# Hybrid attention, mLSTM and Hyena backbone: zero products at the start, the context's rows loaded behind the modulation's weights, the second layer's Hyena filters made first

## The chip, the cores and the metric

The kernel runs on one core of a Trainium2 chip. A core has five engines with an instruction queue each, worked off in order: TensorE (PE, matrix products into PSUM), VectorE (DVE), ScalarE (ACT), GpSimd (POOL) and SyncE (SP, which here only issues DMAs). The metric is the device time of one execution in microseconds (us), lower is better.

## The reference

Two layers over 1024 latent tokens and 256 context tokens of width 1024. Each layer normalises and modulates the tokens (adaLN), projects them once, runs three groups of mixers side by side, projects back, and ends in a convolutional feed-forward network. The parts that the change touches are the modulation (a product of `silu(c)` with `ada_w`), the first norm, the Hyena filters (a small network with sines over a fixed embedding of time, which does not depend on the tokens), and by its place in the queue the gates of the mLSTM.

```
def rmsnorm(x, g):
    y = x * rsqrt(mean(x * x) + EPS) * g
mods = silu(c) @ ada_w + ada_b                  # shift, scale, gate of each norm
h = rmsnorm(x, g) * (1 + scale) + shift         # input of the shared projection
p = h @ w_in                                    # attention | mLSTM | Hyena
filt = sin(freq * (sin(freq * (emb @ w1 + b1)) @ w2 + b2)) @ w3 * window
filt = filt / sum(|filt|)                       # layer L, class of times
x = x + gate * (concat(mla(p), mlstm(p), hyena(p, filt)) @ w_out)
x = x + gate * conv_ffn(norm(x))
```

## The kernel before

Features lie on partitions, tokens on columns, in three blocks: 0 and 1 of 512 latent tokens, 2 of 256 context tokens. A float32 product is carried by three passes on TensorE (`mm3`): values and weights are split into a high and a low part (`wh` and its low half; the pair `B` for tokens), so a tile of 128 features over 8 tiles of the width is 24 products.

The program is written as one sequence, and a scheduler that simulates the engines' times puts every instruction in its place on its engine's queue. What it writes there is fixed: each engine works its queue in order, and an instruction that waits holds up all behind it. `later(by)` gives the filters a priority of some instructions behind their place, so that they fill gaps.

The run begins with `xT` (8 tiles of 128 x 1280, latent and context columns, in tiles `S`) and the constants. Then the modulation of the first norm: 8 groups (4 `nb`, 2 `half`) of four weight tiles of 256 KB in tiles `B` (`ada`, DMA at line 360): 16 products `a<-B,c_cs` (line 365), a copy by ScalarE (`adarow`, 368), small transpositions `a<-c_sel,adarow`, and the sum with the bias by VectorE (`mods`, 373). The last group also gives the scale `A` (376). Beside this, sums of squares (`nacc`, `nsq`) are collected and turned into 1/rms (`rs_v`, `rs_s`, `rs_r`), which `rs_d` and a product `pj<-rs_d,c_ones` spread over the partitions (`nrb`).

`norm` then makes the tiles `B` of each block: two VectorE operations (453, 456) and one of ScalarE (455) for each of 8 tiles. `mixers_in(L)` runs the filters (`filters`, 477; six or four sines of seven steps, 459), the low-rank projection of the queries (tiles Q0 to Q2; products `pk<-B,wh` and `pj<-B,wh`), then the projection MISC, the gates of the mLSTM (`ml_gates`: `mlLI`, `mlLF`, `mlRR`, `mlast`, `mlmrow`, `mldg`, `mlE`, tiles of a pool `rg`), and by heads V and O (`by_token`, products `pk<-wh,B`). The products of the filters are `f<-zemb,hw`, `f<-sn_h,hw` and `f<-hw,sn_h`, their taps `ft` go to DRAM. The pools of the phases follow one another round the same memory.

Of the kernel before, what the change touches and what calls it, by code (L numbers as in the profile page):

```python
# [9 lines left out]
F32 = mybir.dt.float32  # L10
F32R = mybir.dt.float32r
AF = mybir.ActivationFunctionType
ALU = mybir.AluOpType
AX = mybir.AxisListType
PSUM = bass.MemoryType.PSUM
# [7 lines left out]
TP = 1282                     # token axis with a zero after each stream: x 0:1024, 0, ctx 1025:1281, 0  # L23
# [4 lines left out]
# mLSTM heads are kept in the order 0, 2, 1, 3: head i = 2 * half + pair  # L28
HP = [0, 2, 1, 3]
LATER_F = 100                 # priority of the filters, in instructions behind their place  # L30
SBUF_BYTES = 212832            # a partition of SBUF, as far as it is free
# [3 lines left out]
# (first token, columns, stream: 0 latent / 1 context)  # L35
# [3 lines left out]
# --------------------------------------------------------------------------  # L39
# constants that depend on shapes alone  # L40
# --------------------------------------------------------------------------
def _dft(n, step):
    """Cosines and sines of the classes of n times, step apart, at the first n / step frequencies
    k + 1/2 of 2 n: a list of [time, frequency] each."""
# [7 lines left out]
def _consts():  # L52
# [35 lines left out]
    c["dftc"] = np.stack([ec, oc, es, os_, ec.T, oc.T, es.T, os_.T], 1)      # [n][m][k]  # L88
    cs, sn = _dft(NX, 4)
    cl = [0, 2, 1, 3]  # L90
    f = np.stack([np.stack([cs[i], -sn[i] if i == 3 else sn[i]]) for i in cl])      # [class, cs, time, k]
    f = f.reshape(2, 2, 2, 2, 128, 2, 128)                # [pair, class, cs, half, time, kt, k]
    c["dftf"] = f.transpose(5, 0, 4, 1, 2, 3, 6).reshape(2, 2, 128, 1024)
    v = np.stack([np.stack([cs[i].T, sn[i].T]) for i in cl])      # [class, cs, k, time]
    v = v.reshape(2, 2, 2, 2, 128, 256)                   # [pair, class, cs, kt, k, time]
# [4 lines left out]
def _host(inp):  # L100
    """Lay the inputs out for the chip: slices, transposes, replication."""
# [4 lines left out]
    def colmaj(a):                       # [L, n*128] -> [L, 128, n]  # L106
        return a.reshape(a.shape[0], -1, 128).transpose(0, 2, 1)
# [22 lines left out]
    st = np.stack([cols[n] for n in T_TILES], 1)             # [L, tile, D, 128]  # L130
    o["win"] = st.reshape(L, 14, 8, 128, 128).transpose(0, 1, 3, 2, 4).reshape(L, 14, 128, 1024)
    vo = np.stack([w[:, :, 928:1184], w[:, :, 1184:1440]], 1)  # [L, 2, D, 256]
# [20 lines left out]
    def conv(cw, cb):                    # [L,3,C],[L,C] -> [L,128,C/128,4]  # L153
        a = np.concatenate([cw, cb[:, None]], 1)
        return a.reshape(L, 4, -1, 128).transpose(0, 3, 2, 1)
# [4 lines left out]
    qk = np.zeros((L, 2, 2, 128, 128), np.float32)           # [L, pair, q/k, in, out]  # L160
# [9 lines left out]
    o["hyv"] = np.stack([g["hy_b1"], g["hy_b2"], g["hy_sin_freq"]], -1)   # [L,64,3]  # L170
# [3 lines left out]
    wo = wo.reshape(L, 8, 128, 8, 128)               # [L, k, p, m, c]  # L174
    o["wout"] = wo.transpose(0, 3, 2, 1, 4).reshape(L, 8, 128, 1024)
    up = g["ffn_w_up"].reshape(L, 8, 128, 2, N_FF, 128)      # [L, k, p, ab, j, c]
# [13 lines left out]
class Kern:  # L190
# [30 lines left out]
    def rewind(self):  # L221
        """The next pool at the start of the memory that the phases share: the pools follow one
        another round it, so an unused one takes up what is left. No other pool is open there."""
# [19 lines left out]
    def later(self, by):  # L243
        """Scheduled as if traced `by` instructions later: work that fills gaps."""
# [9 lines left out]
    def mm3(self, out, lh, ll, rh, rl, start, stop):  # L254
        """One K tile of a float32 product carried by three float32r passes."""
# [4 lines left out]
    def ps(self, shape=(128, 512)):  # L260
        """The next of the two banks that all phases share."""
# [9 lines left out]
    def bpair(self, b):  # L271
        """hi and lo of one block of tokens; the context block carries a zero at each end."""
# [1416 lines left out]
```

## Time and profile before

| | |
|---|---|
| three runs | 3817.67 us median (3814.6 to 3827.63) |
| the profiled execution | span 3828.4 us, from first to last instruction; the runs beside it took 3814.6 to 3827.63 |
| TensorE | 3547.6 us busy, 93% of the span; mean granted clock 0.961 |
| VectorE, ScalarE, GpSimd | 2001.4, 1294.6 and 923.9 us busy (52%, 34%, 24%) |
| DMA | 319.46 MB, mean 83 GB/s |

Times in the rows below are those of this one execution, from the span's start. Busy shares are means over stages with different bounds; what a stage costs is read in its own windows. In a timeline, the bracket is the engine's idle time just before the instruction, and what ended it. In the names of the order below, the last number tells tiles of one name apart.

### The profile page before, as it was taken

The numbers are of one execution on the slowest core, as the hardware profiler recorded it, in microseconds if no ns is written. First come the engines' busy times: TensorE is split into PE (matmuls) and PEld (weight loads), VectorE is DVE, ScalarE is ACT, GpSimd is POOL, SyncE is SP. The second block draws the span as 40 slices with busy tenths as digits, with TensorE's granted clock in tenths as the row PEclk, the third lists the DMA queues.
The fourth block names the chain that finished last, engine by engine and source line by source line (L and its number), as shares of the span: only waits on it lengthen the run. The fifth ranks groups of instructions, "written<-read, shape, count | busy, mean of one in ns | idle before, by whom it ended". The sixth has DMA issues, their size and how long they took to land.

```text
span 3828.4 us, 45926 instructions
## 1 busy us (share of the span) xinstructions
PE 3547.6 (93%) x17696; PEld 2809.5 (73%) x17696; DVE 2001.4 (52%) x3037; ACT 1294.6 (34%) x2108; POOL 923.9 (24%) x782
## 2 busy tenths in 40 slices
PE   5999869989899999999999799978999999999997
PEld 3798755556677888888888678856666778888885
DVE  5646675445565433434334765566666543444345
ACT  4433314445543221212112443324566432222222
POOL 1402442222311111111112141143334122222221
PEclk8999989989999999999999899889999999999998
DMA  5322544466242111111111222343232311111111
GB/s 176 115 69 90 198 130 141 126 168 170 71 138 66 39 34 39 39 33 34 39 39 39 94 95 88 108 141 105 54 84 80 102 44 44 45 55 45 44 50 66
DMA packets 195007, 319.46 MB, mean 83 GB/s; under 512 B 32207, under 2 KB 112160, under 8 KB 194788
## 3 DMA queue, kind: packets, MB, share of 16 engines
q1 hardware_dynamic: 194244, 316.23, 26.6%
q8 instruction: 139, 2.28, 0.3%
q14 instruction: 80, 0.66, 0.1%
q0 software_dynamic: 544, 0.31, 0.0%
HBM read 263.50 MB, written 52.81 MB: 83 GB/s over the span
## 4 chain that ended last, share of the span: by engine, by line
PE 59%; DVE 6%; DMA 3%; ACT 2%; issue 2%; POOL 1%; SPq 0%; DVEq 0%; ACTq 0%; POOLq 0%
PE u L252 29%; PE pk L252 12%; PE pj L252 12%; PE st L252 2%; PE pv L252 2%; PE hf L252 1%; ACT wh L300 1%; PE mi L252 0%; DVE B L456 0%; DMA vst<-Ph 0%; PE sm L252 0%; DVE sa L453 0%; PE mo L252 0%; DMA B<-mix 0%; DVE S L1515 0%
## 5 line engine op out<-in xcount | busy, mean ns | idle before, releaser
L252 PE MATMUL u<-B,wh 128*128 128x512 f32 (+1 forms) x3240 | 727.0, 376 | 17.6 <-ACT wh L300 10.6
L252 PEld LDWEIGHTS u<-B,wh 128*128 128x128 f32 x3240 | 573.9, 189 | 141.3 <-ACT wh L300 12.7
L301 POOL TENSOR_TENSOR wh<-wr,wh 128x1024 fp32r<-128x1024 f32 x92 | 222.3, 2416 | 1116.1 <-ACT wh L300 1116.1
L300 ACT CAST wh<-wr 128x1024 fp32r<-128x1024 f32 (+2 forms) x188 | 188.8, 1005 | 775.9 <-PE u L252 425.8
L252 PE MATMUL u<-B,wx 128*128 128x512 f32 (+1 forms) x2040 | 435.1, 367 | 2.3 <-DVE sa L1469 2.3
L252 PEld LDWEIGHTS u<-B,wx 128*128 128x128 f32 x2040 | 352.6, 189 | 70.9 <-issue 2.5
L252 PE MATMUL pj<-B,wh 128*128 128x512 f32 (+1 forms) x1644 | 381.8, 378 | 16.2 <-DVE wh L301 7.0
L252 PE MATMUL pk<-B,wh 128*128 128x512 f32 (+1 forms) x1485 | 355.9, 386 | 31.9 <-ACT S L588 7.8
L252 PEld LDWEIGHTS pj<-B,wh 128*128 128x128 f32 x1644 | 288.5, 193 | 83.6 <-issue 11.9
L252 PEld LDWEIGHTS pk<-B,wh 128*128 128x128 f32 x1485 | 265.7, 197 | 102.2 <-issue 15.3
L1515 DVE SCALAR_TENSOR_TENSOR S<-pk,mods,S 128x512 f32<-128x512 f32 (+1 forms) x220 | 152.7, 694 | 322.5 <-PE pk L252 322.3
L1344 POOL TENSOR_TENSOR Pl<-P,Ph 128x512 fp32r<-128x512 f32 (+1 forms) x168 | 219.4, 1306 | 405.9 <-ACT Ph L1343 349.1
L1515 DVE SCALAR_TENSOR_TENSOR S<-pj,mods,S 128x512 f32<-128x512 f32 (+1 forms) x220 | 152.7, 694 | 307.9 <-PE pj L252 307.8
L252 PE MATMUL st<-qh,S 96*128 96x512 f32 (+1 forms) x960 | 292.7, 411 | 15.1 <-DMA qh<-mr 7.9
L1308 DVE TENSOR_REDUCE mx<-sm 128x1 f32<-128x512 f32 (+1 forms) x400 | 227.6, 588 | 116.4 <-PE sm L252 114.1
L1468 DVE SCALAR_TENSOR_TENSOR sa<-u,ffc,sa 128x1281 f32<-128x1281 f32 (+1 forms) x88 | 124.3, 1413 | 276.3 <-ACT sa L1467 275.0
L1342 ACT ACTIVATE P<-st 128x512 f32<-128x512 f32 (+1 forms) x336 | 197.9, 590 | 162.0 <-PE st L252 82.4
L252 PE MATMUL pk<-g,wh 128*128 128x512 f32 (+1 forms) x1032 | 242.2, 370 | 7.7 <-ACT g L283 3.6
L252 PE MATMUL pj<-g,wh 128*128 128x512 f32 (+1 forms) x1032 | 245.1, 370 | 2.7 <-POOL wh L301 1.6
L252 PEld LDWEIGHTS st<-qh,S 96*128 96x128 f32 (+1 forms) x960 | 183.0, 196 | 75.0 <-DMA qh<-mr 12.2
L252 PE MATMUL pv<-Ph,B 128*64 128x512 f32 (+2 forms) x672 | 213.1, 398 | 12.7 <-ACT Ph L1343 8.4
L252 PEld LDWEIGHTS pk<-g,wh 128*128 128x128 f32 x1032 | 179.6, 189 | 43.8 <-DVE S L1515 4.2
(391 smaller groups left out, 5048.5 us busy)
## 6 DMA issues: line engine op xcount, KB each, us to landing
B<-in_adaw_dram SPq DMA_DIRECT2D x192, 256.0 KB
wr<-in_wup_dram SPq DMA_DIRECT2D x88, 512.0 KB
wr<-in_wdn_dram SPq DMA_DIRECT2D x50, 512.0 KB
wr<-in_wout_dram SPq DMA_DIRECT2D x40, 512.0 KB
wr<-in_win_dram SPq DMA_DIRECT2D x28, 512.0 KB
S<-in_xT_dram SPq DMA_DIRECT2D x16, 640.0 KB
mlrb<-rrows SPq DMA_DIRECT2D x36, 256.0 KB
B<-mix SPq DMA_DIRECT2D x32, 256.0 KB
```

Of the source, the lines that this page charges most:

```text
L252: self.nc.tensor.matmul(out, lhsT, rhs, start=start, stop=stop)
L300: self.nc.scalar.copy(hi, wr)
L301: (self.nc.gpsimd if self.wpool else self.nc.vector).tensor_tensor(lo, wr, hi, op=ALU.subtract)
L1308: nc.vector.reduce_max(st["mx"][:, qt, bi:bi + 1], ps[:, :kn], axis=AX.X)
L1342: nc.scalar.activation(P[:, :n], ps[:, :n], AF.Exp, scale=SCALE)
L1344: (nc.gpsimd if j % 2 else nc.vector).tensor_tensor(Pl[:, :n], P[:, :n], Ph[:, :n], op=ALU.subtract)
L1468: nc.vector.scalar_tensor_tensor(y[:, 1:W], pu[:, 0:W - 1], cw[:, 0:1], y[:, 1:W], op0=ALU.mult, op1=ALU.add)
L1515: nc.vector.scalar_tensor_tensor(x, ps, self.mods[L][:, 40 + m, s:s + 1], x, op0=ALU.mult, op1=ALU.add)
```

## The change

- `xT` is loaded in two parts: the latent columns first, the context's columns behind all 32 weight tiles of the modulation, on the same queue.
- `filters(1)` is made at the beginning, ahead of the modulation in the program, with its DMAs on GpSimd's queue and three of each sine's seven steps on GpSimd. `filters(0)` stays in `mixers_in(0)`, but uses the same tiles (pool `rf`), so it comes after `filters(1)`. `mixers_in(1)` has no filters.
- 70 products of a tile of zeros (`wu<-ntmp`) stand ahead of the modulation, and for 7 of the 8 groups two products of ones with the last two of the group's four weight tiles (`wu<-B,c_ones`, 128x256). Nothing reads `wu`.
- In PSUM the modulation has three banks instead of six, the filters two, `wu` one.

```diff
+WARM = 70
...
-    def sine(self, ps, n, freq, b, sp):
+    def sine(self, ps, n, freq, b, sp, eng):
...
-        nc.vector.tensor_scalar(k[:, :n], a[:, :n], 1.0 / (2.0 * math.pi), magic, op0=ALU.mult, op1=ALU.add)
-        nc.vector.tensor_scalar(k[:, :n], k[:, :n], -magic, None, op0=ALU.add)
+        eng.tensor_scalar(k[:, :n], a[:, :n], 1.0 / (2.0 * math.pi), magic, op0=ALU.mult, op1=ALU.add)
+        eng.tensor_scalar(k[:, :n], k[:, :n], -magic, None, op0=ALU.add)
...
-        nc.vector.tensor_scalar(a[:, :n], a[:, :n], 3.1415925, -3.1415925, op0=ALU.min, op1=ALU.max)
+        eng.tensor_scalar(a[:, :n], a[:, :n], 3.1415925, -3.1415925, op0=ALU.min, op1=ALU.max)
...
-    def filters(self, L, sp, pp, tag):
+    def filters(self, L, sp, pp, tag, eng, dma):
...
     def mixers_in(self, L):
-            fp = self.pool(e, f"pf{L}", PSUM, f0=2, ap=1)
-            with ExitStack() as e1, self.later(LATER_F):
-                rp = self.pool(e1, f"rf{L}", sn_a=1, sn_k=1, sn_h=1, hw1=1, hw2=1, hw3=1, hv=1, fb=2, fab=1, ft=1,
-                               fl1=1, fls=1, win=2, zemb=1)
-                self.filters(L, rp, fp, "f0")
+            fp = self.pool(e, f"pf{L}", PSUM, f0=2 if L == 0 else 1, ap=1)
+            if L == 0:
+                with self.erf, self.later(LATER_F):
+                    self.filters(L, self.rf, fp, "f0", nc.vector, nc.sync)
...
     def run(self):
-                nc.sync.dma_start(x[:, :T], a["xT"][k])
+                nc.sync.dma_start(x[:, :NX], a["xT"][k][:, :NX])
...
-                pp = self.pool(e0, "p0", PSUM, a0=6)
+                self.rf = self.pool(e0, "rf", sn_a=1, sn_k=1, sn_h=1, hw1=1, hw2=1, hw3=1, hv=1, fb=2, fab=1,
+                                    ft=1, fl1=1, fls=1, win=2, zemb=1)
+                pp = self.pool(e1, "p0", PSUM, a0=3, f0=2, wu=1)
+                self.hsc = [self.t(self.cp, [128, 2, 2], f"c_hsc{L}") for L in range(DEPTH)]
+                self.filters(1, self.rf, pp, "f0", nc.gpsimd, nc.gpsimd)
+                z = self.t(rp, [128, 512], "ntmp", F32R)
+                nc.gpsimd.memset(z.bitcast(F32), 0.0)
+                wu = self.t(pp, [128, 512], "wu")
+                for i in range(WARM):
+                    self.mm(wu, z[:, 0:128], z)
                 for nb in range(4):
                     for half in range(2):
-                        self.ada(0, nb, half, lambda: self.blk(dt=F32), pp, "a0")
+                        ws = self.ada(0, nb, half, lambda: self.blk(dt=F32), pp, "a0")
+                        for w in ws[2:] if (nb, half) != (3, 1) else ():
+                            self.mm(wu[:, 0:256], self.ones, w[:, 1])
+                for k in range(8):
+                    nc.sync.dma_start(xs[k][:, NX:T], a["xT"][k][:, NX:T])
```

Three places of TensorE's queue. The first is in the modulation, around the products of group 2 (the third of eight). Before, the transposition of a group (`a<-c_sel,adarow`) stands between its products and the next group's:

```order
L252 MATMUL a_38_259<-c_sel_187,adarow_257 128x2 x2
L365 MATMUL a_39_263<-B_270,c_cs_184 32x256 x2
L365 MATMUL a_39_263<-B_268,c_cs_184 32x256 x2
L365 MATMUL a_39_263<-B_266,c_cs_184 32x256 x2
L365 MATMUL a_39_263<-B_264,c_cs_184 32x256 x2
L252 MATMUL pk_516<-c_ones_191,nacc_493 128x2 x4
L252 MATMUL a_45_282<-c_sel_187,adarow_280 128x2 x2
L365 MATMUL a_46_286<-B_293,c_cs_184 32x256 x2
```

Now the products of ones on the weights of groups 5 and 6 (`wu<-B_611`, then `wu<-B_634` and `wu<-B_636`; group 6 has the tiles `B_630` to `B_636`) stand behind group 2's products:

```order
L366 MATMUL a_108_529<-B_536,c_cs_184 32x256 x2
L366 MATMUL a_108_529<-B_534,c_cs_184 32x256 x2
L366 MATMUL a_108_529<-B_532,c_cs_184 32x256 x2
L366 MATMUL a_108_529<-B_530,c_cs_184 32x256 x2
L253 MATMUL wu_408<-B_611,c_ones_191 128x256
L253 MATMUL wu_408<-B_634,c_ones_191 128x256
L253 MATMUL wu_408<-B_636,c_ones_191 128x256
L253 MATMUL a_114_548<-c_sel_187,adarow_546 128x2 x2
L366 MATMUL a_115_554<-B_561,c_cs_184 32x256 x2
L366 MATMUL a_115_554<-B_559,c_cs_184 32x256 x2
L366 MATMUL a_115_554<-B_557,c_cs_184 32x256 x2
L366 MATMUL a_115_554<-B_555,c_cs_184 32x256 x2
```

What moved: behind group 2's products TensorE now takes up weights of group 6, before group 2's transposition and before the products of group 3 (`B_555` to `B_561`) and of all later groups.

The second place is the first projection of layer 0, at the end of the 24 products of tile Q0 on block 0. Before, the products of Q0 and Q1 (there `pk_990` and `pj_1017`) alternate as the tiles `B` come, both to their end:

```order
L252 MATMUL pj_1017<-B_482,wh_986 128x512
L252 MATMUL pj_1017<-B_481,wh_987 128x512
L252 MATMUL pj_1017<-B_487,wh_986 128x512
L252 MATMUL pk_990<-B_488,wh_980 128x512
L252 MATMUL pk_990<-B_487,wh_981 128x512
L252 MATMUL pj_1017<-B_488,wh_986 128x512
L252 MATMUL pj_1017<-B_487,wh_987 128x512
L252 MATMUL f_217_746<-sn_h_744,hw_209_724 64x512
```

Now:

```order
L253 MATMUL pk_1269<-B_765,wh_1260 128x512
L253 MATMUL pk_1269<-B_771,wh_1259 128x512
L253 MATMUL f_66_330<-sn_h_328,hw_28_223 64x512
L253 MATMUL pk_1269<-B_772,wh_1259 128x512
L253 MATMUL pk_1269<-B_771,wh_1260 128x512
L253 MATMUL pj_905<-rs_d_903,c_ones_191 128x256
L253 MATMUL pj_1296<-B_729,wh_1265 128x512
L253 MATMUL pj_1296<-B_730,wh_1265 128x512
```

What moved: the product that spreads the context's 1/rms (`pj_905<-rs_d_903`) stands between Q0 (`pk_1269`) and Q1 (`pj_1296`) of block 0.

The third place is in the gates of layer 0, from the last maxima to the first product of the states. Before, rows of V and O stand between the steps, as here behind the second small product on `mldg`; the first product on `wqk` comes 31 rows later:

```order
L252 MATMUL pk_2280<-wh_2270,B_463 128x256
L252 MATMUL pk_2280<-wh_2271,B_463 128x256
L252 MATMUL pk_2280<-wh_2270,B_464 128x256
L252 MATMUL pk_2280<-wh_2276,B_469 128x256
L252 MATMUL mm_1562<-mldg_1566,c_ones_191 128x128
L252 MATMUL pj_2308<-wh_2270,B_445 128x256
L252 MATMUL pj_2308<-wh_2271,B_445 128x256
L252 MATMUL pj_2308<-wh_2270,B_446 128x256
L252 MATMUL pj_2308<-wh_2270,B_451 128x256
```

Now:

```order
L253 MATMUL mm_1767<-c_ident_189,mlLI_1762 64x128
L253 MATMUL mm_1767<-c_ntri_966,mlLF_1761 64x128 x2
L253 MATMUL mm_1767<-c_ident_189,mlLI_1762 64x128
L253 MATMUL mm_1767<-c_ntri_966,mlLF_1761 64x128
L253 MATMUL mm_1802<-c_ident_189,mlast_1797 1x128 x2
L253 MATMUL mm_1828<-c_ones_191,mlmrow_1807 128x2
L779 MATMUL mm_1836<-c_ident_189,mlRR_1774 128x128 x3
L253 MATMUL mm_1841<-mldg_1842,c_ones_191 128x128
L253 MATMUL mm_1841<-mldg_1845,c_ones_191 128x128
L253 MATMUL mm_2346<-wqk_1872,S_1962 128x128
L253 MATMUL mm_2346<-wqk_1872,S_2057 128x128
L253 MATMUL pk_2615<-wh_2549,B_729 128x256
```

What moved: the products of V and O that stood between the steps are now ahead of them, and from `mm_1767` to `mm_2346` the gates' own products follow one another directly.

## Rows read from the trace of the kernel before

**Rows 1.** Windows: busy us by engine, granted clock, DMA share, GB/s.
```profile
40.00:45.00 5.00, 5.00 (x25) 2.65 (x25) 3.25 (x11) 2.70 (x8) 0.00 (x0) 1.00 1.09 361
```

**Rows 2.** Timeline of PE: start, us, instructions, idle before.
```profile
28.13 1.94 PE L365 MATMUL a<-B,c_cs 128*32 128x256 f32 x16 [5.74 <-DMA B<-in_adaw_dram]
...
47.95 1.07 PE L365 MATMUL a<-B,c_cs 128*32 128x256 f32 x16
...
55.33 0.61 PE L252 MATMUL a<-c_sel,adarow 128*128 128x2 f32 x4 [0.57 <-ACT adarow L368]
```

**Rows 3.** Timeline of DVE around the scale A.
```profile
56.17 0.17 DVE L376 SCALAR_TENSOR_TENSOR A<-mods,ng 128x16 f32<-128x16 f32 x1
...
57.40 2.73 DVE L453 SCALAR_TENSOR_TENSOR ntmp<-S,A,nrb 128x512 f32<-128x512 f32 x4
```

**Rows 4.** Groups of DVE, 58 to 92 us: busy, mean ns.
```profile
L456 DVE SCALAR_TENSOR_TENSOR B<-ntmp,mods,B 128x512 fp32r<-128x512 f32 x16 | 11.3, 738 | 0.0
L453 DVE SCALAR_TENSOR_TENSOR ntmp<-S,A,nrb 128x512 f32<-128x512 f32 x16 | 11.2, 740 | 0.0
...
L469 DVE SCALAR_TENSOR_TENSOR sn_a<-sn_k,sn_a 64x512 f32<-64x512 f32 x5 | 3.4, 677 | 0.0
```

**Rows 5.** Windows of the norm.
```profile
76.00:80.00 4.00, 0.68 (x2) 0.19 (x2) 4.00 (x7) 3.37 (x5) 0.00 (x0) 1.00 0.00 0
```

**Rows 6.** Timeline of PE, layer 0's projections.
```profile
84.84 8.66 PE L252 MATMUL pk<-B,wh 128*128 128x512 f32 x24 [4.45 <-ACT S L588]
...
97.62 1.98 PE L252 MATMUL f<-hw,sn_h 64*128 64x512 f32 x4
...
110.47 5.75 PE L252 MATMUL pk<-B,wh 128*128 128x512 f32 x24
...
169.79 7.21 PE L252 MATMUL pj<-B,wh 128*128 128x512 f32 x24
```

**Rows 7.** Waits of PE, 56 to 300 us: total, times, longest.
```profile
PE f L252 <- ACT sn_h L472: 7.7, 2, 4.0
```

**Rows 8.** Windows, layer 0's gates.
```profile
198.00:228.00 30.00, 29.47 (x246) 28.41 (x245) 14.31 (x57) 7.28 (x13) 1.05 (x2) 1.00 0.16 49
```

**Rows 9.** Timeline of PE, layer 1's gates.
```profile
2278.18 1.40 PE L713 MATMUL mm<-c_ident,S 16*128 16x16 f32 x20
...
2302.08 0.38 PE L252 MATMUL mm<-c_ones,mlmrow 1*128 1x2 f32 x2
...
2306.91 1.22 PE L252 MATMUL mm<-wqk,S 128*128 128x128 f32 x4 [1.10 <-DVE mlE L792]
```

**Rows 10.** Timeline of DVE, layer 1's gates.
```profile
2282.38 0.24 DVE L726 SCALAR_TENSOR_TENSOR mlLF<-mlG,mle 128x80 f32<-128x80 f32 x1 [2.07 <-ACT mle L721]
2285.02 0.42 DVE L738 COPY mlRR<-mm 128x256 f32<-128x256 f32 x1 [2.39 <-PE mm L252]
...
2290.41 0.33 DVE L753 COPY mlast<-mlB 64x1 f32<-64x1 f32 x2
```

**Rows 11.** Timeline of ACT, layer 1's gates.
```profile
2297.23 1.28 ACT L793 ACT_TABLE_LOAD   x1
```

**Rows 12.** Windows 2100 to 2300 us, tile f alone.
```profile
sum 200.00, PE 13.32 PEld 3.79 DVE 8.72; mean PE 4.44 PEld 1.26 DVE 2.91
```

**Rows 13.** Windows of layer 1's beginning, all tiles.
```profile
2100.00:2200.00 100.00, 77.89 (x324) 58.96 (x323) 78.73 (x129) 46.53 (x76) 15.46 (x24) 0.90 0.29 95
2200.00:2250.00 50.00, 47.48 (x206) 33.97 (x206) 38.97 (x46) 21.88 (x31) 26.53 (x24) 0.97 0.40 138
```

**Rows 14.** Waits of PE, 2140 to 2320 us.
```profile
PE f L252 <- ACT sn_h L472: 2.5, 1, 2.5
...
PE mm L252 <- DVE mlE L792: 1.1, 1, 1.1
```

**Rows 15.** Groups of POOL, line 963.
```profile
L963 POOL TENSOR_SCALAR S<-S,c_hyd 128x1280 f32<-128x1280 f32 x2 | 7.3, 3664 | 5.6 <-PE pj L959 5.6
```

**Rows 16.** Groups of DVE, line 600.
```profile
L600 DVE SCALAR_TENSOR_TENSOR S<-S,c_qg,rb 128x512 f32<-128x512 f32 x12 | 12.7, 1101 | 0.0
```

More of the change, by code (lines that the diff above doesn't have):

```diff
@@ L348, in load_consts2 @@
                 nc.gpsimd.dma_start(d[nm], a[nm][L])
-            d["hsc"] = self.t(cp, [128, 2, 2], f"c_hsc{L}")
+            d["hsc"] = self.hsc[L]
             self.lc.append(d)
@@ L377, in ada @@
                                            op0=ALU.add, op1=ALU.mult)
+        return ws
     def inv_rms(self, acc, n, dim, sp, ps):
@@ L484, in filters @@
         hv = self.t(sp, [64, 3], "hv")
-        nc.sync.dma_start(w1, a["hw1"][L])
-        nc.sync.dma_start(w2, a["hw2"][L])
-        nc.sync.dma_start(w3, a["hw3"][L])
-        nc.sync.dma_start(hv, a["hyv"][L])
+        dma.dma_start(w1, a["hw1"][L])
+        dma.dma_start(w2, a["hw2"][L])
+        dma.dma_start(w3, a["hw3"][L])
+        dma.dma_start(hv, a["hyv"][L])
         for blk in (range(3) if L < DEPTH - 1 else range(2)):
@@ L493, in filters @@
             z = self.t(sp, [33, 512], "zemb")
-            nc.sync.dma_start(z[:, :n], a["zemb"][:, c0:c0 + n])
+            dma.dma_start(z[:, :n], a["zemb"][:, c0:c0 + n])
             ps = self.t(pp, [128, 512], tag)
             self.mm(ps[:64, :n], w1, z[:, :n])
-            h = self.sine(ps[:64, :n], n, hv[:, 2:3], hv[:, 0:1], sp)
+            h = self.sine(ps[:64, :n], n, hv[:, 2:3], hv[:, 0:1], sp, eng)
             ps = self.t(pp, [128, 512], tag)
             self.mm(ps[:64, :n], w2, h[:, :n])
-            h = self.sine(ps[:64, :n], n, hv[:, 2:3], hv[:, 1:2], sp)
+            h = self.sine(ps[:64, :n], n, hv[:, 2:3], hv[:, 1:2], sp, eng)
             for i in range(n // 128):
@@ L503, in filters @@
                 win = self.t(sp, [128, 256], "win")
-                nc.sync.dma_start(win, a["hwin"][:, kk])
+                dma.dma_start(win, a["hwin"][:, kk])
                 ps = self.t(pp, [128, 512], tag)
@@ L534, in filters @@
                 nc.vector.reciprocal(v, v)
-                nc.vector.tensor_copy(self.lc[L]["hsc"][:, st], v[:, :, 0])
+                nc.vector.tensor_copy(self.hsc[L][:, st], v[:, :, 0])
     def project(self, L, tiles, blocks):
@@ L1592, in run @@
             self.hs = [{} for _ in range(8)]
-            with ExitStack() as e0:
+            self.erf = e0 = ExitStack()
+            with ExitStack() as e1:
                 rp = self.pool(e0, "r0", nacc=1, nsq=1, ntmp=4, nrb=2, rs_s=2, rs_r=2, rs_v=2, rs_d=1)
-                pp = self.pool(e0, "p0", PSUM, a0=6)
+                self.rf = self.pool(e0, "rf", sn_a=1, sn_k=1, sn_h=1, hw1=1, hw2=1, hw3=1, hv=1, fb=2, fab=1,
[8 more added lines that the diff above has]
+                    self.mm(wu, z[:, 0:128], z)
                 for nb in range(4):
                     for half in range(2):
-                        self.ada(0, nb, half, lambda: self.blk(dt=F32), pp, "a0")
+                        ws = self.ada(0, nb, half, lambda: self.blk(dt=F32), pp, "a0")
[3 more added lines that the diff above has]
+                    nc.sync.dma_start(xs[k][:, NX:T], a["xT"][k][:, NX:T])
                 for b in range(3):
```

## The prediction

> **What bounds the kernel now.** TensorE is busy for nearly the whole span (the table above), so a product that leaves a stretch where TensorE waits for nothing is worth its whole duration, and a product that TensorE does while it would wait anyway costs nothing. The change touches three stretches, and I read them one after the other, first the windows (who is busy), then each engine's timeline (who waits for whom).
>
> The beginning, until 48 us, is bound by the transfer of the first modulation's weights: 361 GB/s with all DMA engines busy [rows 1]. On TensorE the first of eight groups of weight products starts when its weights land, at 28.13 [rows 2]. What the reader is to see there: a group takes 1.94 us at 28.13, but 1.07 at 47.95, the same 16 records. That is the lower of the clock's two levels (1.2 GHz) against the higher (2.4), although the granted clock of this stretch reads 1.00; I go by the durations. TensorE is done with the last transposition at 55.33 + 0.61 = 55.94, and VectorE has the scale `A` at 56.17 [rows 3].
>
> From there to about 92 us VectorE is the bound: it is busy 4.00 of 4.00 us, GpSimd 0.00, TensorE 0.68 [rows 5]; the norm costs it two operations of 0.74 for each 128x512 tile [rows 4]. TensorE works without a break from 84.84 [rows 6].
>
> The gates of layer 0 (198 to 228 us) run through small steps on TensorE, VectorE and ScalarE, and TensorE is busy 29.47 of 30.00 there [rows 8]: V and O products of the heads stand between the steps. The input phase of layer 1 holds its filters, 13.32 us of TensorE [rows 12].
>
> **The change part by part.** *Weights earlier.* The context's 1.05 MB no longer lies ahead of the weights (2.9 us at 361 GB/s [rows 1]), but layer 1's filter data do, some 0.5 MB by its tile sizes (1.5 us). A group of four weights is 1.05 MB, 2.9 us. Before, group 6 of 0 to 7 was in at 28.13 + 6 x 2.9 = 45.5; now, by this, at 44 (43 to 46).
>
> *Zero products and products on weights.* The 70 products on zeros stand ahead of the first weight group, in time that TensorE waits in. They cost nothing unless the first group is delayed; 70 of 128x512 at 0.24 (24 in 5.75 [rows 6]) are 17 us, and the wait for weights is longer. The 14 products on weights are another matter, by the order: two on group 6's weights stand before the transposition of group 2 and before the products of groups 3 to 7. TensorE works in order, so until group 6 has landed it does nothing for those five groups, although their weights are there. From 44 it then owes five groups at 1.07, six transpositions at 0.61, one wait of 0.57 for ScalarE's copy [rows 2], five filter products at 0.99 [rows 6] and about 1.5 for the statistics: 5.4 + 3.7 + 0.6 + 5.0 + 1.5 = 16 us. So the last transposition ends near 60, `A` follows at 61 (before 56.17 [rows 3]): **5 us later** (3 to 8). The warm clock is in this: at the lower level the 16 us would be over 25.
>
> *The context behind the weights.* Its sums of squares and its 1/rms now come after `A`, inside the norm of the latent blocks. In TensorE's order the spreading product `pj_905` of the context stands between Q0 and Q1 of block 0, and waits for VectorE's `rs_d_903`. VectorE has in front of that 29 norm operations at 0.74 [rows 4], three sine steps at 0.68 and some ten small ones: 21.5 + 2.0 + 2.9 = 26.4 us from its first norm operation. That one came 1.2 us after `A` before (57.40 [rows 3]); so 57.4 + 5 + 26.4 = 88.8. Three of seven sine steps go to GpSimd, which idles here [rows 5], and take some 0.4 off VectorE each, but are longer there: 3.66 us for 1280 columns [rows 15], so by estimate 1.5 for 512, thrice in a row per sine. And GpSimd beside VectorE may cost: the same kind of operation as the norm's takes 1.10 instead of 0.74 where other engines work beside it [rows 16]. I take 2 us for this (0 to 8), so Q1 of block 0 starts near 91.3. Before, TensorE ran without a break from 84.84 [rows 6]: 6.5 later, and it still owes Q1 of block 0 (5.75 for 24, in [rows 6]) and six filter products more than before, since layer 0's filters have not begun (5.9): 18.1. Back come the wait for `sn_h` of 4.0 [rows 7] and the cold stretch at 169.79 (7.21 instead of 5.75, [rows 6]): 5.5. **Layer 0's projections lag by 12.5 us** (5 to 22).
>
> The Trainium skill, SBUF — State Buffer, section "Who interferes with whom", says that a VectorE instruction with two inputs in SBUF contends with a GpSimd instruction that reads SBUF, through one shared pair of ports held for the whole instruction. The norm's operations and the sine's subtractions have two such inputs. Rows 16 against rows 4 agree in sign but do not show who worked beside them. By that rule the third rival below would come about.
>
> *Layer 0's gates.* Layer 0's filters now come second in the same buffers and end later, while the V and O products go ahead as before. The gates' tiles lie in the filters' memory and wait for their end. So in the new order most of V and O is done when the gates begin: after the transpositions come 21 V and O rows, and then every step of the gates, one behind another, with nothing between until `wqk`. The chain is to be seen bare in layer 1: 3.0 us from the transpositions' end to `mlLF`, 5.7 from `mlRR` to the last maximum's copy [rows 10], 4.8 from `mlmrow` to the first `wqk` product [rows 9], about 1.3 for the sums between and 5.5 for the row's steps (of 11.3 there, where weight conversions and queued products stood between): 20.3, and 2.3 for the exponential, the output gate and one more table load of 1.28 [rows 11] until the bank is free. Off go 2.5 for the 21 rows (half of 5.75 x 21/24) and 4.5 for the chain's own products: 15.5 us without work. Then the clock is cold: 24 products take 8.66 instead of 5.75 [rows 6], 2.9. **18 us lost** (12 if the first links run ahead, 24 if the whole 27.3 us of layer 1 recur less the 21 rows).
>
> *Layer 1 without filters.* Its products lie where TensorE is busy: 13.3 us off [rows 12], and the wait of 2.5 for `sn_h` [rows 14]. Its gates' four waits, the largest 1.1 [rows 14], 3.2 together, go because V and O now stand around them, and about 1 of the tail: **20 us won** (16 to 25).
>
> Sum: 12.5 + 18 - 20 = +10.5 us. The profiled execution spans 3828.4, 10.7 above the median of the runs, 3817.67; I add the difference to the median: **3828**.
>
> **The rivals.** *Not slower: layer 1 gives more* (faster). In layer 1's beginning TensorE is busy only 77.89 of 100 us and VectorE 78.73 [rows 13]. If VectorE is the bound there, what leaves it (8.7 us that read the filters' products [rows 12], twelve subtractions of 0.68 [rows 4] and smaller steps, about 20) counts too, and layer 1 gives up to 33 instead of 20. With the smaller lag of 5 and a stall of 13 in layer 0's gates that is 5 + 13 - 33 = -15: 3803. It decides where layer 1's gain exceeds the two losses by 11.5: over 29.5 with these, over 42 with the losses as worked out above. Against it: TensorE is busy 47.48 of 50.00 us where most of the filters stand [rows 13], so only the early part can give more.
> *The losses cancel* (same): the lag shrinks to 5 because TensorE's later work had waits to take it up: 5 + 15 - 20 = 0, 3818.
> *GpSimd and VectorE hold each other up* (slower): six to nine GpSimd steps lie within the norm, and each holds it up for its 1.5 us: 9 to 13, of which 2 are in the sum, so about 3837. For it [rows 16], against it that an instruction loses at most the rest of the other's time.
> *The clock falls* while TensorE waits for group 6 (slower): the 16 us become about 26, 3838. The products on weights are there against it; before, the stretch was cold [rows 2].
>
> **How the numbers follow.** What a measurement of this kernel can tell from no change is about 0.3%, 11.5 us, and my sum lies just at that border. I give the forecast 0.52, half on each side of the border; faster 0.21; the losses cancel 0.10; contention 0.09; a cold clock 0.08. So faster 0.21, same 0.36, slower 0.43. The range of 8 in 10 reaches from the faster rival's end to beyond the slower ones: 3801 to 3846; the forecast's own is 3819 to 3838.
>
> **What would show it.** Right: `A` at 60 to 63; TensorE without a break from about 91; one idle stretch of 14 to 20 us in layer 0's gates near 220, with the small products one by one in it; layer 1's beginning 16 to 25 shorter. Wrong, each by itself: `A` before 57 (weights not gating); V and O products between the gates' steps; norm operations over 0.9 (contention); layer 1 shorter by 30.

## The result and the profile after

The changed kernel takes 3855.7 us, median of 4 runs (3840.73 to 3859.08), the kernel before in the 4 runs beside it 3822.61, 33.1 less by these medians. The ratio is 1.0078 (95% interval 1.0061 to 1.0094): **slower by 0.8%**. Its profiled execution, 3838.5 us of span, is the fastest of the four, so one pair of profiles understates the difference. Runs of both kernels unchanged, on other chips (e1, e7, e13, e17, e18 below), give three profiles of the changed kernel and four of before. The times at which TensorE begins certain products divide them into stages:

| stage on TensorE | before, four profiles | changed, three | difference of means |
|---|---|---|---|
| start to first score product (`st`), layer 0 | 534.9, 539.3, 535.3, 535.0 | 577.8, 584.9, 582.3 | +45.6 |
| to first feed-forward product (`u`): attention | 647.6, 639.0, 642.9, 652.6 | 644.1, 656.4, 649.6 | +4.5 |
| to the end of layer 0's last `u` | 988.6, 988.8, 988.7, 989.0 | 990.9, 989.1, 989.1 | +0.9 |
| to first `st` of layer 1 | 414.5, 417.7, 414.5, 412.9 | 384.8, 383.3, 383.3 | -31.1 |
| to TensorE's last product | 1233.5, 1230.2, 1231.7, 1233.7 | 1231.7, 1239.6, 1235.2 | +3.2 |

The sum is +23.1, the difference of the mean spans 22.9; the times by themselves, by the three ratios to before (1.0078, 1.0081, 1.0057), give 22 to 31. Attention differs by more among profiles of one kernel (639 to 653) than between the kernels. So the case is two numbers: 46 lost until layer 0's attention, 31 won at the start of layer 1.

The beginning, TensorE's timeline of the changed kernel's first profile:

```profile
5.83 9.58 PE L253 MATMUL wu<-ntmp 128*128 128x512 f32 x32 [5.83 <-POOL ntmp L1605]
...
25.25 1.07 PE L366 MATMUL a<-B,c_cs 128*32 128x256 f32 x16
...
37.56 1.93 PE L366 MATMUL a<-B,c_cs 128*32 128x256 f32 x16
...
51.20 1.07 PE L366 MATMUL a<-B,c_cs 128*32 128x256 f32 x16
...
62.66 0.61 PE L253 MATMUL a<-c_sel,adarow 128*128 128x2 f32 x4
64.12 1.48 PE L253 MATMUL pj<-rs_d,c_ones 128*128 128x512 f32 x2 [0.85 <-DVE rs_d L399]
78.41 0.98 PE L253 MATMUL pk<-c_ones,nacc 128*128 128x2 f32 x4 [12.81 <-DVE nacc L437]
82.07 6.80 PE L253 MATMUL pk<-B,wh 128*128 128x512 f32 x22 [2.67 <-DVE rs_v L390]
...
95.70 1.22 PE L253 MATMUL pj<-rs_d,c_ones 128*128 128x256 f32 x2 [5.17 <-DVE rs_d L399]
97.38 2.93 PE L253 MATMUL pj<-B,wh 128*128 128x512 f32 x6 [0.46 <-ACT nrb L404]
...
105.32 4.35 PE L253 MATMUL pk<-B,wh 128*128 128x512 f32 x18
```

The zero products run from 5.83 until the first weights are in, and seven of the eight groups take 1.07 (the one at 37.56 takes 1.93; the first in [rows 2] 1.94): in this profile the clock is at its higher level for most of the modulation. Yet the last transposition ends at 63.27 (55.94 in [rows 2]). A product on the context's squares stands ahead of the first projection and waits 12.81 for them. Q0 of block 0 is done at 90.53; then TensorE waits 5.17 for the context's `rs_d`, Q1 of block 0 comes at 97.38, and Q0 of block 1 at 105.32, in [rows 6] at 84.84. VectorE beside it, the scale and the first norm operations:

```profile
67.03 0.15 DVE L377 SCALAR_TENSOR_TENSOR A<-mods,ng 128x16 f32<-128x16 f32 x1
...
67.44 5.30 DVE L455 SCALAR_TENSOR_TENSOR ntmp<-S,A,nrb 128x512 f32<-128x512 f32 x4
```

`A` is 10.9 later than in [rows 3], and the first four norm operations take 5.30, there 2.73. The groups of the norm, with mean ns:

```profile
L455 DVE SCALAR_TENSOR_TENSOR ntmp<-S,A,nrb 128x512 f32<-128x512 f32 x16 | 14.2, 917 | 0.0
L458 DVE SCALAR_TENSOR_TENSOR B<-ntmp,mods,B 128x512 fp32r<-128x512 f32 x16 | 13.4, 868 | 0.0
```

They are 0.92 and 0.87 against 0.74 in [rows 4]: 32 operations, 4.9 us (2.4 in e1 and e17). V and O begin 12.4 later than before, here the first rows of before and of the changed kernel:

```profile
187.38 1.70 PE L252 MATMUL pk<-wh,B 128*128 128x256 f32 x13
```

```profile
199.77 0.99 PE L253 MATMUL pk<-wh,B 128*128 128x256 f32 x7
```

Then the filters of layer 0 that are still owed, and the gates. First the windows from there to the attention, of before and then of the changed kernel: all tiles, then the products of tile `f` alone; behind them the waits of TensorE in the gates:

```profile
187.38:534.90 347.52, 320.84 (x2045) 278.83 (x2044) 220.44 (x392) 109.34 (x221) 103.05 (x110) 0.95 0.35 113
187.38:534.90 347.52, 0.56 (x4) 0.52 (x4) 0.15 (x1) 0.95 0.35 113
```

```profile
199.77:577.79 378.02, 335.07 (x2064) 284.94 (x2063) 237.56 (x421) 118.52 (x233) 118.44 (x125) 0.92 0.33 109
199.77:577.79 378.02, 8.53 (x24) 3.35 (x24) 5.33 (x10) 0.92 0.33 109
```

```profile
PE mm L253 <- DVE mlast L754: 5.9, 1, 5.9
PE mm L253 <- DVE mlmrow L766: 4.0, 1, 4.0
PE f L253 <- POOL fl L521: 2.2, 1, 2.2
PE mm L253 <- DVE mlLF L727: 1.6, 1, 1.6
PE mm L253 <- DVE mlE L793: 1.1, 1, 1.1
PE mm L253 <- DVE mlTT L780: 0.6, 1, 0.6
...
PE mm L253 <- DVE mldg L784: 0.4, 1, 0.4
PE mm L779 <- DVE mlast L769: 0.2, 1, 0.2
```

The gates' waits are 13.9 (5.9 + 4.0 + 1.6 + 1.1 + 0.6 + 0.4 + 0.2, rounded rows), one behind another as the order has them; in [rows 8] TensorE was idle for 0.5 there. Windows of the gates, with the granted clock:

```profile
240.00:290.00 50.00, 36.10 (x303) 32.77 (x304) 23.91 (x81) 12.10 (x25) 5.59 (x13) 0.80 0.24 76
```

So from V and O to the attention, of 30.5 in all: 8.0 of filter products (8.5, before 0.6), 13.9 of waits in the gates, 2.2 of waiting for the filters' sum, and some 6 because the other products run longer (TensorE is busy 14.2 more, of which 8.0 are the filters'), at a granted clock of 0.92 instead of 0.95; in the gates it is 0.80.

In layer 1, from the last products of layer 0's feed-forward to the first score, sums of before and then of the changed kernel:

```profile
sum 436.40, PE 393.42 PEld 323.78 DVE 276.77 ACT 151.04 POOL 121.71; mean PE 131.14 PEld 107.93 DVE 92.26 ACT 50.35 POOL 40.57
```

```profile
sum 406.80, PE 370.24 PEld 313.50 DVE 242.27 ACT 137.75 POOL 95.71; mean PE 123.41 PEld 104.50 DVE 80.76 ACT 45.91 POOL 31.90
```

TensorE is busy 23.2 us less, of which the filters' products are only 13.3 [rows 12]. The other 9.9 are products that run shorter: the windows' granted clock, weighted by their lengths, is 0.93 instead of 0.91. And it is idle 6.4 less (36.6 against 43.0). Both recur: over this stage the granted clock is 0.91 to 0.93 in the four profiles of before, 0.93 to 0.94 in the three of the changed kernel.

### The profile page after: what moved, and what is told of

It is laid out like the page before. It is cut to its first block, busy times and chain, and to the rows that moved or that the text cites. A ratio compares the mean times of both kernels' runs of the same rounds, so it can differ in the third digit from the quotient of the medians.

```text
span 3838.5 us, 46110 instructions
## 1 busy us (share of the span) xinstructions
PE 3566.8 (93%) x17794; PEld 2830.0 (74%) x17794; DVE 2003.0 (52%) x3025; ACT 1297.7 (34%) x2109; POOL 951.5 (25%) x809
## 5 line engine op out<-in xcount | busy, mean ns | idle before, releaser
L253 PEld LDWEIGHTS pk<-B,wh 128*128 128x128 f32 x1485 | 264.7, 197 | 89.7 <-issue 11.1
L253 PE MATMUL pv<-Ph,B 128*64 128x512 f32 (+2 forms) x672 | 214.6, 400 | 12.2 <-ACT Ph L1344 8.2
L253 PEld LDWEIGHTS pj<-g,wh 128*128 128x128 f32 x1032 | 180.6, 189 | 42.2 <-POOL wh L302 5.6
```

What stands on the lines that cost most here:

```text
L253: self.nc.tensor.matmul(out, lhsT, rhs, start=start, stop=stop)
```

## Experiments

Ratios are to the kernel before, run beside them. Edits are to the changed kernel where they say "changed", else to before.

**e1, e17: the changed kernel again; e7, e13, e18: before again.** 

> The changed kernel again, unchanged. Its profiled execution (3840.73 us, clock 0.957) was the fastest of four, the others 3853 to 3859 at 0.954 and 0.955. Theory 'clock': the stalls of the start (about 12 us) and of layer 0's gates (about 16 us) recur within 1 us in every execution, layer 1 gives back 18, and what separates 3841 from 3856 lies in stretches in which TensorE's granted clock falls, attention above all; executions then order by clock. Rival 'start': the slow executions are later already at 300 us, by another 10 to 15 us. Rival 'chance': it comes out at 3825 to 3840 this time and the difference of the medians was chance.

> The changed kernel, unchanged, beside the kernel before on one chip. Sum by stage against the yardstick beside it: first score product +42 to +50, layer 1 from the feed-forward's end to its first score product -28 to -31, so +13 to +20 from these. If the two attentions make up the rest of the 30 us, layer 0's is 6 to 14 us longer than the yardstick's, layer 1's with the feed-forward 3 to 8. If they are equal within 3 us, the rest lies elsewhere or the first difference of medians was too large.

e1: 1.0081 (1.0066 to 1.0096); e17: 1.0057 (1.0037 to 1.0076). Before again gave 0.9993, 0.9988 and 0.9990. The stages are in the table above. On e17's chip, against the yardstick e18 beside it: +47.3 until the scores, -3.0 in attention, -29.6 in layer 1's first part, +1.5 to the end, +16. I had expected an attention 6 to 14 longer; it is not, so a loss in attention is not shown, and by my own condition the rest lies elsewhere or the first difference of medians was too large.

The stretch from V and O to the scores recurs: 378.0, 378.3 and 377.7 us in the three profiles of the changed kernel (347.5 to 352.2 before), with 13.9 to 14.0 of waits in the gates. What varies is the start: V and O begin at 199.8, 206.6 and 204.6 (185.3 to 187.4 before). In e1 the clock falls within the modulation: the last three groups take 1.9 again, and four filter products behind the first of these 3.77 instead of 1.98:

```profile
50.99 1.91 PE L366 MATMUL a<-B,c_cs 128*32 128x256 f32 x16
```

`A` comes at 72.9 there; in e17, where the last two groups take 1.93, at 71.3. Between the first profile and e1 attention differs by 12.3 too, so neither 'clock' nor 'start' alone makes the difference between these two. For before alone I had expected:

> The kernel before, unchanged, for a second profile of it. If the attention of layer 0 (a stretch with many waits and a clock that falls and rises) takes different times in executions of one program, this profile shows it: from the first score product to the first product of the feed-forward 640 to 660 us, where the first profile has 647.5. If it is 647 within 2 us here too, the 656 of the changed kernel's second profile are a consequence of the change. Time 1.000 of before.

Attention spread over 639.0 to 652.6 in one program. A difference of that size between two single profiles says nothing.

**e9: layer 1's filters first, and nothing else but the PSUM banks for them (four for the modulation instead of six).**

```diff
+                self.filters(1, self.rf, pp, "f0", nc.gpsimd, nc.gpsimd)
                 for nb in range(4):
...
+                with self.erf, self.later(LATER_F):
+                    self.filters(L, self.rf, fp, "f0", nc.vector, nc.sync)
```

> The kernel before with layer 1's filters made first (GpSimd steps and DMA queue as in the change), and nothing else: no zero products, no products on weights, the context loaded with the rest. In its order the gates of layer 0 again stand bare behind layer 0's filters. Theory 'filters': this part brings the whole loss in layer 0 (first score product 35 to 43 us later than before) and the whole gain in layer 1 (25 to 30 us); time +10 to +25. Rival 'the rest costs it': without zero products and late context the time is within 5 us of before.

1.0056 (1.0037 to 1.0075), as the whole change. First score at 578.2 (+42 against the mean of before), layer 1's stage 382.9 (-32). Both halves of the result are in this one edit. Its beginning, without zero products, is slower still: `A` at 69.4. GpSimd's sine steps in its timeline:

```profile
22.75 0.61 POOL L468 TENSOR_SCALAR sn_k<-sn_a 64x512 f32<-64x512 f32 x1 [2.94 <-DVE sn_a L465]
23.45 1.51 POOL L469 TENSOR_SCALAR sn_k<-sn_k 64x512 f32<-64x512 f32 x1
...
81.36 5.03 POOL L472 TENSOR_SCALAR sn_a<-sn_a 64x512 f32<-64x512 f32 x1 [8.84 <-DVE sn_a L471]
93.23 4.89 POOL L468 TENSOR_SCALAR sn_k<-sn_a 64x512 f32<-64x512 f32 x1 [6.84 <-DVE sn_a L465]
```

The same step takes 0.61 while VectorE does little (22.75) and 4.89 in the norm (93.23). The Trainium skill, SBUF — State Buffer, section "Who interferes with whom", names the lock that a VectorE instruction with two SBUF inputs and a GpSimd instruction that reads SBUF share; these rows agree, and here it is mostly GpSimd that waits: 5 us in a chain on which layer 0's filters hang. In the changed kernel itself the sine steps take 2.72 at most, and the slowest step of GpSimd is one of the filters' sums, here before the norm and then in it:

```profile
61.72 0.72 POOL L520 TENSOR_TENSOR fl<-fl,fab 128x256 f32<-128x256 f32 x1 [0.46 <-ACT fab L515]
...
74.10 8.42 POOL L520 TENSOR_TENSOR fl<-fl,fab 128x256 f32<-128x256 f32 x1 [3.23 <-ACT fab L515]
```

It recurs with 8.42 in e1 and e17.

**e19: changed, all sine steps on VectorE.**

```diff
-                self.filters(1, self.rf, pp, "f0", nc.gpsimd, nc.gpsimd)
+                self.filters(1, self.rf, pp, "f0", nc.vector, nc.gpsimd)
```

> The changed kernel with all sine steps on VectorE, nothing else changed. In its order layer 0's filters end some 95 rows earlier on TensorE, and 36, 39 and 48 rows stand between the gates' first steps; only the last ones stay bare. If GpSimd's slow steps are what makes the filters late, the idle time in the gates falls from 14 to 4 to 7 us and the first score product comes 8 to 15 us earlier than in the changed kernel: time -8 to -15 against it. If VectorE is the bound of the norm, its added steps (three of 0.4 for each of four sines) delay the norm by as much, and no more than 4 us are won.

1.0029 (1.0017 to 1.0042), 8.9 us below e17's median on the same chip. Waits of TensorE around its gates:

```profile
PE mm L253 <- DVE mlE L793: 1.1, 1, 1.1
PE mm L253 <- DVE mlast L754: 1.1, 1, 1.1
PE mm L253 <- DVE mldg L784: 0.8, 1, 0.8
PE mm L253 <- DVE mlTT L780: 0.7, 1, 0.7
...
PE mm L779 <- DVE mlast L769: 0.3, 1, 0.3
```

4.0 in the gates, not 13.9, and the first score 15.5 earlier than in e17, although `A` comes at 76.5, later than in any other run. V and O begin at 209.2 (204.6 in e17), and from there to the scores it is 357.6 instead of 377.7 (before 349.5 in the mean). So the loss behind V and O goes with the end of layer 0's filters, 28 in e17 and 8 here; the other 23 of this run lie ahead of V and O. Whether the filters end earlier by GpSimd's slow steps or by the other order that the scheduler made of them is not separated.

**e11, e15: layer 0's filters first, layer 1's in their old place, the context's rows ahead of the weights as before; e15 with the zero products and those on weights.** The lines against the changed kernel:

```diff
-                self.filters(1, self.rf, pp, "f0", nc.gpsimd, nc.gpsimd)
+                self.filters(0, self.rf, pp, "f0", nc.vector, nc.gpsimd)
...
             if L == 0:
-                with self.erf, self.later(LATER_F):
-                    self.filters(L, self.rf, fp, "f0", nc.vector, nc.sync)
+                self.erf.close()
+            else:
...
+                    self.filters(L, rp, fp, "f0", nc.vector, nc.sync)
```

> Layer 0's filters made at the beginning (all sine steps on VectorE, DMAs on GpSimd's queue), layer 1's in their old place in layer 1; no zero products, context loaded with the rest. If the late end of layer 0's filters is what bares the gates, V and O products stand between the gates' steps here, the stall of 14 us is gone, and about 9 us of filter products lie in the beginning, where TensorE waits: first score product 5 to 12 us earlier than before, time -4 to -12. Rival: VectorE is the bound of the beginning, the filters' steps delay the norm by their own time, and nothing is gained (0 to +8).

> Layer 0's filters at the beginning and layer 1's in layer 1, as in the run without zero products, now with the 70 products on zeros and the 14 on weights. There the clock was at its lower level from 50 us on, filter products took 1.9 us instead of 1.0, and the scale A came near 73. If the clock is what delays A, A comes at 60 to 66 here and the time falls by 4 to 10 us against that run (which was 5.8 us above before): within 5 us of before. If the filters' chain of waits delays A, it stays over 70 and the time does not fall.

e11: 1.0011 (0.9999 to 1.0023); e15: 0.9993 (0.9981 to 1.0005). In their order V and O stand between the gates' steps again. The waits of TensorE in e11's gates, all that there are:

```profile
PE mm L253 <- DVE mlast L758: 2.1, 1, 2.1
PE pk L253 <- ACT S L680: 0.6, 1, 0.6
PE pk L253 <- DVE wh L302: 0.5, 2, 0.3
PE mm L253 <- DVE mlLF L731: 0.3, 1, 0.3
```

The bared gates are gone, and with them the loss behind V and O: from there to the scores 349.9 and 350.8 (before 349.5). The first score comes at 544.4 and 543.5, 8 and 7 later than before, nearly all of it ahead of V and O. My gain of 5 to 12 at the start did not come: `A` at 73.3, and at 68.3 with zero products, between what the two readings for e15 said. Neither beats before beyond its interval.

**e2: changed, without the products on weights.**

```diff
-                        for w in ws[2:] if (nb, half) != (3, 1) else ():
-                            self.mm(wu[:, 0:256], self.ones, w[:, 1])
```

> The changed kernel without the 14 products on the modulation's weights; the 70 products on zeros stay. If these 14 hold up groups 3 to 7, the scale A comes at 57 to 60 instead of 67 and the time falls by 5 to 9 us against the changed kernel. If they keep the clock up and only that counts, the modulation's groups take 1.9 instead of 1.07 us and A does not come earlier; time unchanged within 4 us. The stall in layer 0's gates (14 us idle) stays in either case.

1.0082 (1.0066 to 1.0098), as e1 beside it. `A` comes at 65.3 instead of 72.9, although from 32.88 on the groups take 1.93: so the products on weights do hold `A` back. Already group 1 starts at 28.99 here, at 37.17 in e1. And nothing is won: TensorE then stands 16.84 at the context's squares, and the first projection starts at 89.4 (88.8 in e1). Rows of TensorE, GpSimd and VectorE:

```profile
85.02 1.01 PE L253 MATMUL pk<-c_ones,nacc 128*128 128x2 f32 x4 [16.84 <-DVE nacc L437]
```

```profile
69.12 7.29 POOL L468 TENSOR_SCALAR sn_k<-sn_a 64x512 f32<-64x512 f32 x1 [4.39 <-DVE sn_a L465]
```

```profile
79.34 1.21 DVE L471 SCALAR_TENSOR_TENSOR sn_a<-sn_k,sn_a 64x512 f32<-64x512 f32 x1 [3.41 <-POOL sn_k L469]
```

A sine step of GpSimd takes 7.29 here, most of it within the norm, and VectorE waits 3.41 for the one behind it. The context's `rs_d` comes only 2.2 earlier than in e1, and Q1 of block 0 with it.

**e6: changed, both filters at their old places. e4: only the context behind the weights.**

> The changed kernel with both layers' filters at their old places (in the input phases, all sine steps on VectorE); zero products, products on weights and the context behind the weights stay. In its order V and O products stand between the gates' steps of layer 0 again. Theory: the gates' stall (16 us) goes, layer 1's gain (about 18 us) goes too, and the start's lag shrinks; so 3825 to 3834 us, 20 us or more below the changed kernel's median. Rival 'start bears it all': the loss stays at 25 us or more.

> The kernel before with nothing but the context's columns loaded behind the modulation's weights. The scale A comes 2 to 4 us earlier (1.05 MB less ahead of the weights), but VectorE collects the context's squares inside the norm of the latent blocks, so the norm ends 2 to 5 us later relative to A. Theory: these cancel, within 5 us of before. Rival: TensorE stands behind the context's statistics, as in the changed kernel (12.8 us of wait there), and layer 0's projections come 6 to 12 us later.

e6: 1.0020 (1.0003 to 1.0036); e4: 1.0017 (1.0002 to 1.0032). Two rows of e6's TensorE timeline:

```profile
49.01 0.61 PE L253 MATMUL a<-c_sel,adarow 128*128 128x2 f32 x4 [0.57 <-ACT adarow L369]
...
70.01 1.01 PE L253 MATMUL pk<-c_ones,nacc 128*128 128x2 f32 x4 [16.32 <-DVE nacc L437]
```

Here zero products, products on weights and late context do what the start of the change seems made for: `A` at 49.9, 6.3 earlier than before. Then TensorE waits 16.32 for the late context, and V and O begin at 187.9 as before. With the filters at their old places both halves of the result are gone: first score at 537.8 (534.9 to 539.3 before), layer 1's stage 414.7. In e4 `A` comes at 61.1, not earlier, and V and O begin 9.6 later than before, as the rival said, but not by its wait: TensorE waits 3.22 and 5.29 for ScalarE's copies in the modulation.

**e5, e14: only the 70 zero products, twice.** 

> The kernel before with nothing but the 70 products on zeros ahead of the modulation (modulation with 5 PSUM banks). If the zero products bring the clock up early, groups of the modulation take 1.07 instead of 1.9 us, but most of that is hidden behind the transfer of the weights: A earlier by 2 to 4 us, time -2 to -4, no change that can be measured. Rival: the clock is down again at the first wait for weights, A at 56 as before, 0 us. Slower by over 5 us would mean that the products stand in the way.

> The kernel before with nothing but the 70 products on zeros, a second time: it was 14 us slower than before the first time, and no stage of its profile up to the attention showed more than 5. If the zeros cost something by what they change in the order of later instructions, the same stages are longer here, against the yardstick beside it: 2 to 6 us in the mLSTM's states, 5 to 12 in layer 0's attention; time +10 to +16. If the first result was chance, within 4 us of before.

1.0038 (1.0024 to 1.0052) and 1.0028 (1.0014 to 1.0043): slower. `A` comes at 59.3 and 56.2, not earlier, as the rival said: the zero products end before the first weights are in, TensorE waits, and the first group is at the clock's lower level again, here in e14:

```profile
26.99 1.93 PE L365 MATMUL a<-B,c_cs 128*32 128x256 f32 x16 [4.96 <-DMA B<-in_adaw_dram]
```

The loss is not where the products are: e14's first score comes 0.8 after its yardstick's, e13. Attention, first score to first `u`, in windows of e13 and then of e14:

```profile
sum 643.00, PE 570.55 PEld 404.62 DVE 350.76 ACT 302.76 POOL 162.70; mean PE 95.09 PEld 67.44 DVE 58.46 ACT 50.46 POOL 27.12
```

```profile
sum 654.00, PE 581.57 PEld 411.69 DVE 348.60 ACT 303.51 POOL 164.53; mean PE 96.93 PEld 68.61 DVE 58.10 ACT 50.59 POOL 27.42
```

11 us more of busy time for the same products, 654 in both runs. But e18, before unchanged, has 652.6 there at the same granted clock, 0.92, so the attention is not shown to be the place. The scheduler has put some later instructions in another order; that this order costs the time was not tried, and e15, with the same zero products, has 639 in attention. Where e5 and e14 lose stays open.

**e12: changed, banks of their own for layer 0's filters.**

```diff
-            fp = self.pool(e, f"pf{L}", PSUM, f0=2 if L == 0 else 1, ap=1)
             if L == 0:
                 with self.erf, self.later(LATER_F):
-                    self.filters(L, self.rf, fp, "f0", nc.vector, nc.sync)
+                    ff = self.pool(self.erf, "pfil", PSUM, f0=2)
+                    self.filters(L, self.rf, ff, "f0", nc.vector, nc.sync)
+            fp = self.pool(e, f"pf{L}", PSUM, f0=1, ap=1)
```

> The changed kernel, with PSUM banks of their own for layer 0's filters, so that the gates' bank is not one that the filters still use. In its order the transpositions stand 28 rows earlier, ahead of the filters' last products, and 31 rows of V and O and the filters stand between them and the next gates' step; from the maxima on the steps stay bare. If the bank alone holds the gates up, the idle time in the gates falls from 14 to 3 us or less; if the filters' memory in SBUF holds them (tiles of the gates lie there), only the first waits go and 8 to 12 us stay. Time against the changed kernel -10, or -2 to -5.

1.0124 (1.0100 to 1.0148), a miss, and worse: now the low-rank queries' products (`ap`) begin at 239.89, directly behind the filters' last at 239.01, so the gates began at 260.8 instead of 243.7 and stayed bare. It says nothing on which of the two memories holds the gates; that stays open.

**e16: before, with layer 1's filters beside layer 0's gates.**

```diff
...
+                if L == 0:
+                    rf = self.pool(e1, "rf1", sn_a=1, sn_k=1, sn_h=1, hw1=1, hw2=1, hw3=1, hv=1, fb=2, fab=1, ft=1,
+                                   fl1=1, fls=1, win=2, zemb=1)
+                    ff = self.pool(e1, "pg1", PSUM, f0=2)
                 self.ml_gates(misc, ra, rg, pp)
+                if L == 0:
+                    with self.later(LATER_F):
+                        self.filters(1, rf, ff, "f0")
```

> The kernel before with layer 1's filters made in layer 0 beside the gates, behind layer 0's own, in memory and banks of their own; beginning as before, no zero products, context with the rest. If the explanation holds (layer 1 gives 28 to 31 us back when its filters are gone, and layer 0 loses because its own filters end late and the gates stand bare), layer 0 loses only the 13 us of products and some 5 to 10 of waits in the filters' chain, and layer 1 gives 28 to 31: time -5 to -15, faster than both kernels. If the gain in layer 1 hung on the other edits, or the gates are bared here too, 0 to +10.

1.0031 (1.0020 to 1.0041), a miss. Layer 1 won its 28 (stage 384.6), but layer 0 lost 33 until the scores: 17 of filter products, not 13, and 14 of waits in the filters' chain, not 5 to 10. The waits:

```profile
PE f L252 <- POOL fl L519: 7.7, 1, 7.7
PE f L252 <- ACT sn_h L472: 6.4, 2, 4.5
```

## Why the prediction was wrong

The direction and the three places were right, the sizes were not: 3828 forecast, 3855.7 measured, outside the range. Of the signs of being wrong that it named, two came: norm operations over 0.9 (0.92, for one of the two kinds) and layer 1 shorter by 30 (31.1).

- *The start.* `A` 5 later: it came 10.9 (first profile) to 16.7 later (e1). The reason given, products on later groups' weights, is real (e2: without them `A` is 7.6 earlier), and TensorE came to group 6's weights at 44.26, as worked out. From there it took 19.0 instead of 16 to the last transposition, and VectorE's steps for the filters and the sums put `A` 3.8 behind that. In e1 and e17 the clock fell on the way, which is the fourth rival in part, though not while TensorE waited for group 6. From VectorE's first norm operation to the end of the context's `rs_d`, 28.2 us, it went as worked out (26.4 and 2 of contention; 57.4, 5 and these make 90.8, and the 0.5 up to the 91.3 of the prediction has no row). The wait for the context's squares ahead of Q0 had no price in the sum; by these rows it costs nothing, since Q1 waits for `rs_d` anyhow.
- *The lag of layer 0's projections*, 12.5: V and O began 12.4 later in the first profile, 17.0 in the mean of three. The 12.4 is luck: Q0 of block 1 was 20.5 late, not 12.2, and 8.1 came back by V and O, where the sum, with 5.9 more owed and 5.5 back, had nothing come back. **This is the step that failed:** I charged six filter products, 5.9, ahead of V and O, and nothing behind, although I had written that layer 0's filters end later. In fact 8.0 us of their products and 2.2 of waiting came behind V and O, on top of the gates, and of the 4.0 us of `sn_h` wait that I gave back, 2.1 stayed.
- *The gates*, 18: 13.9 idle (15.5 forecast) and some 6 by a lower clock (2.9 forecast), about as worked out. e9 alone brings the loss, e6 takes it away, and e11 and e15 show its cause: with layer 0's filters early the long waits are gone, 2.4 us are left in e11 (2.1 + 0.3). That the gates wait for the filters' memory in SBUF, as the prediction has it, is not shown (e12). Until the scores the two terms made +45.6, not 30.5: 17.0 ahead of V and O, 28.5 behind.
- *Layer 1*, 20 won: 31. Products (13.3) and waits (6.4 less idle; 6.7 forecast) were right; 10 us by a higher clock were not in the sum. The first rival's 33 is near in number, but not by its reason, VectorE as the bound: the rows give 23.2 to TensorE's own busy time and 6.4 to its waits.
- *GpSimd against VectorE*, third rival: real, but smaller on VectorE, 4.9 us on the norm's operations in the first profile and 2.4 in e1 and e17, not 9 to 13. GpSimd lost more: its steps of 8.42 beside operations of 0.74 are far over "the rest of the other's time" that the prediction held against this rival.
- The sum of the errors, 15.1 lost and 11.1 won, and 8.6 in stages that vary by as much, is what separates 10.5 from 23, the difference of the mean profiles.

## What to carry to other kernels

Work that is moved into an idle stretch at the front is not free when what follows it uses the same buffers: ask what now ends last there, and which later chain waits for that end. Here the moved filters cost layer 0 more than they gave layer 1, because layer 0's own filters became second, and the gates behind them lost the products that had covered their steps. Where a scheduler sets the order, an edit that should cost nothing in its place can still cost time (e5 and e14), and one pair of profiles does not show where: attention of before alone spreads over 13.6 us. A stage table over several profiles of both kernels is worth more.

## What the runs showed of the hardware

- One GpSimd operation on 64x512 took 0.61 us at 22.75 and 5.03 and 4.89 us in the norm (e9), where the estimate in the prediction was 1.5. One on 128x256 took 0.72 us at 61.72 and 8.42 in the norm (changed kernel, e1, e17).
- The same program's attention took 639.0 to 652.6 us in four profiles of before, at granted clocks from 0.93 (639.0) to 0.92 (652.6).
- Zero products that run until the first weights are in leave the clock at its higher level: the first modulation group took 1.07 us at 25.25 in the changed kernel, 1.94 at 28.13 in [rows 2]. Where 4.96 us of waiting lay between (e14), it took 1.93.
